# Ending a scatter kernel on Pool: a semaphore wait and a reset of the DMA bookkeeping in place of a drain

## The chip, the cores and the metric

One core of a Trainium2 chip. The time is the device time of one execution, in microseconds (us), median of several executions; the profile's span is 1.8 to 2.2 us shorter than the time of the same execution.

The engines are named as in the profile: PE (TensorE), DVE (VectorE), ACT (ScalarE), Pool (GpSimd) and SP (SyncE); a q after the name is the engine's sequencer. A DMA raises its semaphore, a counter, when it is complete; "landing" in this text is the moment at which an engine's wait for that semaphore is met. The "tail" is the time from the last scatter's landing to the end of the program.

## The reference

```python
def reference(x, scores):               # x: 8 x 2048 x 2560 f32, scores: 8 x 2048 f32
    order = np.argsort(scores, axis=1)
    ranks = np.argsort(order, axis=1)
    out = np.zeros_like(x)
    out[np.arange(B)[:, None], ranks, :] = x
    return out
```

Every row of 10 KB is moved to the place that its score's rank gives it: 168 MB read, 168 MB written, hardly any arithmetic.

## The kernel before

Ranks are counted on VectorE. Most rows go through SBUF: Pool issues a load of 256 rows and, once their ranks are there, two indirect scatters of 128 rows each. The first 256 rows of six batches, and a few others, go straight from DRAM to DRAM in copies of one row, issued by SP and ACT in hardware loops. All synchronization is by hand inside one critical section:

```python
with tc.tile_critical(no_gpsimd_drain=True):
    ...
    def scatters_done(line, k):                  # `line` (an engine) waits for group k's scatters
        i = k % NBUF
        for j in range(GROUPS[BULK[k][1]][1]):
            line.wait(s_scat[i][j], 16 * n_scat[i][j])
    ...
    # SP and ACT: row copies in loops, then each waits for its own
    for line in (sp, act):
        line.wait(s_rows[line], 16 * n_rows[line])
    ...
    for k, (b, g) in enumerate(BULK):            # Pool: 58 groups
        if k >= LAG and k + NBUF - LAG < len(BULK):
            scatters_done(pl, k - LAG)
            load_ahead(k + NBUF - LAG)
        pl.wait(*loaded[k])
        pl.after(dve, t_bulk[b, g])
        for j in range(GROUPS[g][1]):
            scatter(k, j)
    nc.gpsimd.drain()

    for k in range(max(0, len(BULK) - NBUF), len(BULK)):
        scatters_done(sp, k)
```

At the end of the section SP tells the other engines, waits for a drain of ACT, DVE and PE and for a no-op of Pool, and an epilogue with two barriers follows. On Pool that epilogue holds three more drains: a plain one, one with a reset flag over semaphore numbers 132 to 138 (the last not counted, so six numbers), and a plain one.

## Time and profile before

| | before |
|---|---|
| time, median of the first 3 runs | 775.31 us (775.0 to 775.73) |
| span of the profiled run | 772.8 us |
| DMA, mean over the span | 414 GB/s |
| last packet of Pool's DMA queue ends | 770.10 us |
| SP's wait for the last scatter is met | 770.58 us |
| Pool's drain ends | 771.92 us |
| end of the program | 772.80 us |

The first three rows are from the runs and the page; the others are times from the span's start in the trace, in the order in which they end the program. The prediction shows the page's lines and how they are read. What matters is that the DMA engines are full until 766, and that the last 2.23 us (772.801 - 770.575), from the landing of the last scatter to the end, move no data.

### The profile page before, as it was taken

What the parts mean: (1) busy time and instruction counts of PE and PEld (TensorE: products, weight loads), DVE (VectorE), ACT (ScalarE), POOL (GpSimd) and SP (SyncE); (2) the same over time, 40 slices, a digit from 0 to 9 for tenths busy, and PEclk for the clock granted to TensorE, in tenths of its full rate; (3) what the DMA queues carried; (4) which work ended last, traced back from release to release, by engine and by line L of the source; (5) the groups of instructions that cost most, each with busy time, mean ns of one, the idle gap of its engine ahead of it and who ended that gap; (6) DMA issues with size and microseconds to landing.
All of it is one profiled execution on the core that took longest, in us unless ns stands there. A gap on an engine that the chain in (4) does not pass through costs nothing.

```text
span 772.8 us, 8228 instructions
## 1 busy us (share of the span) xinstructions
PE 36.2 (5%) x172; PEld 30.4 (4%) x172; DVE 400.7 (52%) x828; ACT 0.0 (0%) x1; POOL 164.6 (21%) x213
## 2 busy tenths in 40 slices
PE   4000020020020020030000000000000000000000
PEld 3000010010010010030000000000000000000000
DVE  5999979979979979979999500000000000000000
ACT  0000000000000000000000000000000000000000
POOL 4114223222213131312112121212121212112100
PEclk8555555555555555565555555555555555555555
DMA  8999999999999999999999999999999999999996
GB/s 358 418 418 420 418 418 418 418 417 418 418 420 417 420 417 417 419 417 419 416 421 421 422 416 426 416 427 417 422 417 424 417 426 415 424 418 424 419 414 283
DMA packets 80898, 320.15 MB, mean 414 GB/s; under 512 B 28968, under 2 KB 54568, under 8 KB 54568
## 3 DMA queue, kind: packets, MB, share of 16 engines
q0 software_dynamic: 29376, 300.82, 91.7%
q1 hardware_dynamic: 25904, 10.93, 5.2%
q10 hardware_dynamic: 25600, 8.24, 4.3%
q14 instruction: 17, 0.14, 0.0%
q8 instruction: 1, 0.02, 0.0%
HBM read 168.49 MB, written 168.43 MB: 436 GB/s over the span
## 4 chain that ended last, share of the span: by engine, by line
DMA 63%; DVE 13%; another core or an unknown queue 9%; POOL 6%; issue 4%; PE 1%; POOLq 0%; SPq 0%
DMA out_dram<-x,rank_i 57%; DVE trash L239 12%; DMA x<-in_x_dram 6%; POOL out_dram L424 4%; POOL x L126 2%; PE ps_all L196 0%; DVE s_all L341 0%; DMA s_in<-in_scores_dram 0%; PE ps_col L175 0%; POOLq L448 0%; DVE rank_i L277 0%; DVE rank L271 0%; DVE rank L265 0%; PE ps_row L300 0%
## 5 line engine op out<-in xcount | busy, mean ns | idle before, releaser
L239 DVE TENSOR_SCALAR_CACHE_REDUCE trash<-s_all,s_col 128x1792 bf16<-128x1792 f32 (+7 forms) x240 | 315.2, 1348 | 4.6
L424 POOL DMA_INDIRECT out_dram<-x,rank_i x116 | 113.4, 977 | 139.6 <-issue 35.0
L126 POOL DMA_DIRECT2D x<-in_x_dram x88 | 49.4, 565 | 436.9 <-DMA out_dram<-x,rank_i 418.5
L239 DVE SCALAR_TENSOR_TENSOR trash<-s_all,s_col,mask 128x256 bf16<-128x256 f32 x128 | 61.6, 482 | 0.0
L196 PE MATMUL ps_all<-ident,s_col 128*128 128x128 f32 x128 | 28.1, 411 | 3.2 <-DVE s_all L341 2.8
L300 PE MATMUL ps_row<-ident,rank 128*1 128x128 f32 x28 | 8.3, 398 | 393.6 <-DVE rank_i L286 386.4
L196 PEld LDWEIGHTS ps_all<-ident,s_col 128*128 128x128 f32 x128 | 26.5, 222 | 4.2 <-DVE s_all L341 3.2
L341 DVE COPY s_all<-ps_all 128x512 f32<-128x512 f32 x32 | 20.2, 685 | 1.5 <-PE ps_all L196 1.1
L239 DVE DVE_READ_ACCUMULATOR trash<-s_all,s_col 128x1 f32 x240 | 19.9, 83 | 0.0
L300 PEld LDWEIGHTS ps_row<-ident,rank 128*1 128x1 f32 x28 | 2.0, 97 | 397.9 <-DVE rank_i L286 389.5
L311 DVE TENSOR_SCALAR thin_i<-ps_row 1x8 int32<-1x8 f32 x8 | 1.2, 154 | 19.0 <-PE ps_row L300 19.0
L239 DVE DVE_READ_ACCUMULATOR trash<-s_all,s_col,mask 128x1 f32 x128 | 10.7, 83 | 0.0
L326 DVE TENSOR_SCALAR rows_i<-ps_row 1x256 int32<-1x256 f32 x6 | 2.5, 412 | 4.1 <-PE ps_row L300 4.1
L183 DVE COPY s_col<-ps_col 128x128 f32<-128x128 f32 x1 | 0.3, 293 | 4.7 <-PE ps_col L175 4.7
L175 PE MATMUL ps_col<-ident,s_in 8*128 8x8 f32 x16 | 2.1, 262 | 3.9 <-DMA s_in<-in_scores_dram 3.9
L286 DVE TENSOR_SCALAR rank_i<-rank,hole 128x2 int32<-128x2 f32 x8 | 2.1, 262 | 0.3
L175 PEld LDWEIGHTS ps_col<-ident,s_in 8*128 8x128 f32 x16 | 2.0, 211 | 3.9 <-DMA s_in<-in_scores_dram 3.9
L277 DVE CAST rank_i<-rank 128x16 int32<-128x16 f32 (+3 forms) x11 | 1.9, 173 | 0.4
L271 DVE TENSOR_TENSOR rank<-rank,acc 128x16 f32<-128x16 f32 (+3 forms) x11 | 1.9, 171 | 0.4
L265 DVE TENSOR_TENSOR rank<-acc,acc 128x16 f32<-128x16 f32 (+3 forms) x11 | 1.9, 170 | 0.4
L156 POOL TENSOR_SCALAR_AFFINE_SELECT mask<-mask 128x256 f32<-128x256 f32 x2 | 0.8, 398 | 0.0
L168 DVE MEMSET acc<- 128x128 f32 x1 | 0.2, 165 | 1.1 <-SPq L102 1.1
(10 smaller groups left out, 1.8 us busy)
## 6 DMA issues: line engine op xcount, KB each, us to landing
x<-in_x_dram POOLq DMA_DIRECT2D x62, 1280.0 KB
x<-in_x_dram POOLq DMA_DIRECT2D x26, 2560.0 KB
out_dram<-in_x_dram ACTq DMA_DIRECT2D x800, 10.0 KB
out_dram<-in_x_dram SPq DMA_DIRECT2D x800, 10.0 KB
x<-in_x_dram SPq DMA_DIRECT2D x2, 1280.0 KB, 9.1
out_dram<-x,rank_i POOLq DMA_INDIRECT x116, 49.0
s_in<-in_scores_dram SPq DMA_DIRECT2D x1, 64.0 KB
```

What stands on the lines that cost most here:

```text
L126: line.eng.dma_start(out=xb[k % NBUF][:, part], in_=rows[:, part]).then_inc(sem, 16)
L175: nc.tensor.transpose(out=ps_col[:, B * c:B * (c + 1)], in_=s_in[:, r + j:r + m * P:m], identity=ident[:B, :B],)
L196: nc.tensor.transpose(out=ps_all[:, P * c:P * (c + 1)], in_=s_col[:, c, b:b + 1].to_broadcast([P, P]), identity=ident[:],)
L239: do(out=trash[i][:, :P * (hi_c - lo_c)], in0=s_all[:, P * lo_c:P * hi_c], accum_out=acc[i][:, col:col + 1], **how,)
L265: nc.vector.tensor_tensor(out=rank[:, cols], in0=acc[0][:, cols], in1=acc[1][:, cols], op=OP.add)
L271: nc.vector.tensor_tensor(out=rank[:, cols], in0=rank[:, cols], in1=acc[2][:, cols], op=OP.add)
L277: nc.vector.tensor_copy(out=rank_i[:, cols], in_=rank[:, cols])
L286: nc.vector.tensor_scalar(out=rank_i[:, cols], in0=rank[:, cols], scalar1=hole[:, i:i + 1], scalar2=None, op0=OP.add,)
L300: nc.tensor.transpose(out=ps_row[:1, P * j:P * (j + 1)], in_=rank[:, col:col + 1], identity=ident[:],)
L326: nc.vector.tensor_scalar(out=rows_i[b][:].rearrange("o (p j) -> o p j", p=P), in0=ps_row[:1, :WIDE].rearrange("o (j p) -> o p j", p=P), s ...
L341: nc.vector.tensor_copy(out=s_all[:, 512 * q:512 * (q + 1)], in_=ps_all[:, 512 * q:512 * (q + 1)],)
L424: nc.gpsimd.indirect_dma_start(out=out_flat, out_offset=bass.IndirectOffsetOnAxis(ap=rank_i[:, col:col + 1], axis=0), in_=xb[k % NBUF][:, ...
```

## The change

The intent: Pool's drain is still at work when everything has landed. So let Pool wait on the scatters' semaphores itself, and then only reset its DMA bookkeeping.

```diff
             for j in range(GROUPS[g][1]):
                 scatter(k, j)
-        nc.gpsimd.drain()
-
         for k in range(max(0, len(BULK) - NBUF), len(BULK)):
-            scatters_done(sp, k)
+            scatters_done(pl, k)
+
+        nc.gpsimd.dma_reset()
```

The rest of the diff puts the body of the row-copy loop in a function, so that it could be unrolled for the batches of a tuple `FLAT`; `FLAT = ()`, so no batch is, and the instructions are the same. In the built program the reset is a drain instruction with a reset flag over semaphore numbers 96 to 256, that is 160 numbers.

More of the change, by code (lines that the diff above doesn't have):

```diff
@@ L63 @@
     G = 16
+    FLAT = ()
     THIN = {**{(b, 4): 48 for b in range(1, B)}, (7, 5): 44}
@@ L391, with copies @@
                 half = WIDE // 2
-                with line.eng.Fori(0, half // G) as q:
+                def copies(q):
+                    first = b * N + GROUPS[0][0] + half * h
                     _, at = nc.values_load_multi_w_load_instructions(
@@ L402 @@
                     for i in range(G):
-                        row = b * N + GROUPS[0][0] + half * h + i
                         line.eng.dma_start(
                             out=out_bytes[bass.ds(at[i], ROW)],
-                            in_=x_bytes[bass.ds(q * (G * ROW) + row * ROW, ROW)],
+                            in_=x_bytes[bass.ds(q * (G * ROW) + (first + i) * ROW, ROW)],
                         ).then_inc(s_rows[line], 16)
+                if b in FLAT:
+                    for q in range(half // G):
+                        copies(q)
+                else:
+                    with line.eng.Fori(0, half // G) as q:
+                        copies(q)
                 n_rows[line] += half
```

## The prediction

> **What bounds the kernel now.** I read the page first, to see which resource is full and over which part of the span; then the windows of the last microseconds, to see when the data stops; then the few instructions of the epilogue, by their source lines, because the change touches nothing else.
>
> ```profile
> span 772.8 us, 8228 instructions
> DMA  8999999999999999999999999999999999999996
> GB/s 358 418 418 420 418 418 418 418 417 418 418 420 417 420 417 417 419 417 419 416 421 421 422 416 426 416 427 417 422 417 424 417 426 415 424 418 424 419 414 283
> q0 software_dynamic: 29376, 300.82, 91.7%
> HBM read 168.49 MB, written 168.43 MB: 436 GB/s over the span
> ```
>
> The sixteen DMA engines are at nine tenths or more in 38 of 40 slices of 19.3 us, moving a steady 415 to 425 GB/s. DVE is busy 52% and Pool 21%; neither limits anything after the first tenth. The only slices below that are the first (358, the start) and the last (283, the end). A change at the very end can win only in the last slice. The windows there show core time, then five engines' busy time (nothing runs), the clock, the DMA share and GB/s:
>
> ```profile
> 765.50:766.00 0.50, 0.00 (x0) 0.00 (x0) 0.00 (x0) 0.00 (x0) 0.00 (x0) 0.50 0.83 348
> 766.00:766.50 0.50, 0.00 (x0) 0.00 (x0) 0.00 (x0) 0.00 (x0) 0.00 (x0) 0.50 0.29 123
> ...
> 769.50:770.00 0.50, 0.00 (x0) 0.00 (x0) 0.00 (x0) 0.00 (x0) 0.00 (x0) 0.50 0.05 20
> 770.00:770.50 0.50, 0.00 (x0) 0.00 (x0) 0.00 (x0) 0.00 (x0) 0.00 (x0) 0.50 0.00 0
> ```
>
> Full rate lasts until 766.0, a few late DMA engines until 770.0, and then nothing moves: 772.8 - 770.0 = 2.8 us of the span lie behind the last byte. That is all the change can address. What fills those 2.8 us, from the answers on the source lines of the waits on SP (L28), of Pool's drain (L448), of the end of the critical section (L102) and of the program's end (L477); columns: times, duration in ns as min/median/max, first and last start:
>
> ```profile
> L28 SPq EVENT_SEMAPHORE  x8: 27/28/28, 749.6 to 770.6; - x8
> L448 POOLq DRAIN  x1: 32437/32437/32437, 739.5 to 739.5; - x1
> L102 SPq EVENT_SEMAPHORE  x3: 17/28/28, 770.8 to 771.0; - x3
> L102 POOLq NOP  x1: 13/13/13, 772.0 to 772.0; - x1
> L102 SPq NOP  x1: 18/18/18, 772.0 to 772.0; - x1
> L477 POOLq DRAIN  x3: 34/47/72, 772.1 to 772.5; - x3
> L477 PEldq EVENT_SEMAPHORE  x2: 51/51/51, 772.3 to 772.8; - x2
> SPq L102 <- POOLq L102: 0.9, 1, 0.9
> DMA to landing us min/median/max: 29.6/29.6/29.6
> ```
>
> SP's last wait for a scatter is met at 770.6; the last line agrees, since the last scatter was issued at 740.97 and landed 29.6 us later, at 770.6. Pool's drain began at 739.48 (the start that the chain of waits gives for L448) and took 32.437 us, so it ends at 771.92. That is 1.3 us after the last scatter's semaphore was already complete. SP is then the one that waits: 0.9 us for Pool's no-op at the end of the section, from about 771.1 to 772.0. So the drain, not the transfer and not SP, releases the epilogue, and the epilogue from that no-op to the end takes 772.8 - 772.0 = 0.8 us.
>
> **What the Trainium skill says.** "Perfetto Trace Analysis", section "Sequencer-only Instruction (DRAIN, etc)": the profiler's start of such an instruction comes once its semaphores are satisfied, so a recorded duration is execution, not a semaphore wait. This drain has no semaphore, and its 32.4 us are the drain waiting by its own means for what Pool has queued. "PSUM — Partial Sum Buffer", section "Engine vs sequencer instructions": "drain waits for the engine to go fully idle"; the trace agrees as far as it ends only after the last scatter. "DMA: Bandwidth & Descriptors", section "Anatomy of one DMA — SWDGE (gpsimd) path": the semaphore follows only once the last write is confirmed, and this receipt is most of a fixed cost of about 2 us. Here the last bytes are on the DMA engines before 770.0 and the semaphore is seen at 770.6, so the part visible at the end is 0.6 us or little more; the change doesn't touch it. "VectorE: DVE Perf Modes", section "The DRAIN you can't avoid", calls the boilerplate drains some 12 ns on all engines; the trace has 7 to 17 ns on SP, ACT, PE and DVE, but 34 to 72 on Pool, so I use the trace's. No page says what a reset of Pool's DMA bookkeeping costs.
>
> **The change part by part.** The loops over groups, the loads, the scatters and the DRAM-to-DRAM copies are not altered: the tuple of unrolled batches is empty, so every batch takes the loop as before, and the instruction counts on every engine's listing agree but for the epilogue.
>
> Removed: Pool's 32.4 us drain. It lies beside the last transfers but for its last 1.3 us.
>
> Moved: the waits for the last sixteen scatter semaphores go from SP to Pool. In the built program they are eight wait instructions, with the last condition attached to the reset. SP needed 28 ns each, Pool's waits elsewhere show 17 ns. Seven of the eight are met early or with the one that arrives last; at most two or three follow the last landing: 2 to 3 x 17 = 34 to 51 ns, call it 0.05 us. Last semaphore 770.6, so the reset starts at 770.65.
>
> Added: the reset. In the built program it is a drain instruction with a reset flag, over the semaphore numbers 96 to 256. The kernel before already has one such instruction, with the same flag and only the numbers 132 to 138, between its two final barriers: the 72 ns one of Pool's three at L477, against 47 and 34 for the plain ones. If the cost doesn't hang on the range, the reset ends at 770.65 + 0.07 = 770.72.
>
> Freed early: SP no longer waits for scatters, only for its own copies. ACT's copies were complete at 762.1 with the last one issued at 733.2; SP's last was issued at 736.4, so by the same 28.9 us it is through at about 765.3 (an estimate from those rows). The 0.4 us in which SP tells the other engines (770.6 to 771.0) then lies before the last landing, so Pool's no-op finds its condition met. Allow 0.1 us for the branch and fetch between reset and no-op, as from 771.92 to 772.0 now: no-op at 770.82, and the unchanged 0.8 us follow: 771.6.
>
> Sum with a cheap reset: 772.8 - 771.6 = 1.2 us of the span saved, which is 772.0 -> 770.8 at the no-op. The runs' time is longer than the span (775.31 against 772.8, though of different executions), and I take the difference as unchanged.
>
> **The rivals.** (1) The reset costs by the semaphore. The flagged drain took about 72 - 40 = 32 ns more than the plain ones for 6 numbers, 5.3 ns each if all of the difference is due to them; 160 numbers are then 0.85 us. The end would be 0.8 us later than above, a saving of 0.35 us: 774.95. For it speaks only that difference; against it, a second instruction (the range clear, also 72 ns) writes the semaphores themselves. (2) The tail of the drain is real work that has to be done, taking back the ring entries of the scatters, and the reset or the next plain drain does it after all: 1.3 us come back, and the saving is nil or slightly negative, 775.3 to 775.6. For it speaks that the drain ends 1.3 us after all semaphores are in, so it learns of completion in another way; nothing in the trace says whether that is a slow look or work. (3) The drain, while it waits, slows the DMA engines, and its removal speeds up the last 30 us. Against: in the windows from 745 to 765 the DMA share is 1.02 to 1.03 at 408 to 424 GB/s, the same as the 1.02 and 421 from 700 to 720. No gain there. (4) The late DMA engines between 766 and 770 set the end, and their distribution shifts from run to run: that is noise of a fraction of a microsecond, in either direction; the three runs span 775.0 to 775.73, nearly as much as the whole effect.
>
> **Range and chances.** I give 55% to the full 1.2 us, 25% to the half-way reset (0.35), 20% to nothing: 0.66 + 0.09 + 0 = 0.75, and I lean a little toward the full case, the likeliest single one: 0.9 us, so 775.31 - 0.9 = 774.4. The range joins the full saving with a lucky run (774.1 - 0.9 = 773.2) to no saving with an unlucky one (775.8). A change of 2% is 15.5 us; the end has 2.8 us in all to win, so faster by that is next to impossible, 0.5%; slower by it needs a reset of over 16 us, for which nothing speaks but that no page or row bounds it: 1.5%. Within 2%: 98%.
>
> **What would show it.** The page up to the last slice is the same: mean 414 GB/s, DMA-bound. Pool has no drain of tens of microseconds; its waits end with the last landing, 0.6 us or so after the last DMA packet; a reset of about 0.07 us follows, SP is waiting for Pool's no-op since about 766, and from the last landing to the end there are 1.0 us instead of 2.2. A reset of 0.8 us proves rival 1; one of 1.3 us or more, or a long plain drain after it, rival 2. If the GB/s of the last two slices change, rival 3 is at work. The prediction is wrong if the reset takes several microseconds, or if the span falls by more than those 2.8 us.

## The result, and the profile after

| | before | changed |
|---|---|---|
| time, median of 4 runs | 775.2 us | 774.58 us (774.22 to 774.81) |
| span of the profiled run | 772.80 us | 772.35 us |
| wait for the last scatter met | 770.58 us | 771.09 us |
| from there to the end | 2.226 us | 1.260 us |

The ratio is 0.9990, 95% interval 0.9973 to 1.0008. Ratios here are the mean time of one kernel's fast runs over that of the other's fast runs of the same rounds, so not quite the ratio of the medians quoted. An execution counts as slow when it lies over 1.5% above the fastest of its kernel; none here did. Within 2%, and by this interval alone not told apart from no change at all.

The page is the same except at its end (span, DMA share and GB/s in 40 slices, mean):

```profile
span 772.4 us, 8228 instructions
DMA  8999999999999999999999999999999999999997
GB/s 356 420 417 419 417 418 420 417 416 417 420 413 418 418 419 417 418 418 418 417 422 418 424 417 424 416 425 418 426 417 424 417 422 420 420 422 421 420 416 301
DMA packets 80898, 320.15 MB, mean 415 GB/s; under 512 B 28968, under 2 KB 54568, under 8 KB 54568
```

The windows at the end of the changed kernel (same columns as in the prediction):

```profile
769.50:770.00 0.50, 0.00 (x0) 0.00 (x0) 0.00 (x0) 0.00 (x0) 0.00 (x0) 0.50 0.05 20
770.00:770.50 0.50, 0.00 (x0) 0.00 (x0) 0.00 (x0) 0.00 (x0) 0.00 (x0) 0.50 0.05 20
770.50:771.00 0.50, 0.00 (x0) 0.00 (x0) 0.00 (x0) 0.00 (x0) 0.00 (x0) 0.50 0.00 0
```

In this execution the last bytes moved half a microsecond later than in the traced one of before, so the spans differ by less than the tails. The epilogue by source lines, for the waits (L28), the reset (L461), the end of the section (L105), the program's end (L487), and what SP waited for:

```profile
L28 POOLq EVENT_SEMAPHORE  x8: 17/43/43, 751.0 to 771.1; - x8
L461 POOLq DRAIN  x1: 296/296/296, 771.2 to 771.2; - x1
L105 POOLq NOP  x1: 13/13/13, 771.5 to 771.5; - x1
L105 SPq NOP  x1: 18/18/18, 771.6 to 771.6; - x1
L487 POOLq DRAIN  x3: 40/58/64, 771.6 to 772.1; - x3
SPq L105 <- DMA out_dram<-in_x_dram: 31.6, 1, 31.6
SPq L105 <- POOLq L105: 16.6, 1, 16.6
```

The 32 us drain is gone. The eight waits are on Pool, a drain-with-reset of 296 ns follows, and SP has nothing left but to wait 16.6 us for Pool. From the last landing: 0.087 us to the reset's start, 0.296 the reset, 0.044 to Pool's no-op, 0.833 to the end, together 1.260. Before, the same stretch was 1.344 to the end of the drain, 0.045 to the no-op, 0.837 to the end, together 2.226. The tail is 0.97 us shorter.

Twelve runs (seven edited kernels, one of them twice, and both given kernels twice more) then asked three things: is the drain's part after the last landing work or a late look; what does the reset's price hang on; and does the saving in the tail reach the time? All twelve gave correct results.

### The profile page after: what moved, and what is told of

It is laid out like the page before. It is cut to its first block, busy times and chain, and to the rows that moved or that the text cites. A ratio compares the mean times of both kernels' runs of the same rounds, so it can differ in the third digit from the quotient of the medians.

```text
span 772.4 us, 8228 instructions
## 1 busy us (share of the span) xinstructions
PE 35.7 (5%) x172; PEld 30.4 (4%) x172; DVE 400.4 (52%) x828; ACT 0.0 (0%) x1; POOL 165.2 (21%) x213
## 4 chain that ended last, share of the span: by engine, by line
DMA 38%; DVE 37%; another core or an unknown queue 11%; POOL 4%; issue 3%; PE 3%; POOLq 0%; SPq 0%
DVE trash L242 34%; DMA out_dram<-x,rank_i 32%; DMA x<-in_x_dram 6%; POOL out_dram L434 3%; PE ps_all L199 2%; DVE s_all L344 2%; POOL x L129 1%; PE ps_row L303 1%; DMA s_in<-in_scores_dram 0%; PE ps_col L178 0%; DVE rank_i L280 0%; DVE rank L274 0%; DVE rank L268 0%; DVE rank_i L289 0%
```

## The experiments

### Is it the drain itself? A plain drain after the waits, and nothing at all

```diff
 # late_drain
-        nc.gpsimd.dma_reset()
+        nc.gpsimd.drain()
```

> Pool waits for the last scatters as in the changed kernel, then does the old plain drain in place of the reset. Theory A (the drain's 1.3 us after the last semaphore is work that it owes for the queued scatters, taking back their ring entries): the drain still takes 1.0 to 1.4 us after the last landing, the stretch from the last wait's end to the end of the program is about 2.2 us as before, and the time is that of the kernel before, 775.2. Theory B (the drain merely looks late, because it watches by its own means; once all has landed there is nothing to do): it takes 0.03 to 0.1 us, the stretch is 1.0 to 1.1 us, 774.4.

```diff
 # no_reset
-        nc.gpsimd.dma_reset()
```

> Pool waits for the last scatters and then does nothing: no reset and no drain. If the reset's 296 ns are a cost of its own, they go: from the last wait to the end 0.92 us instead of 1.22, 774.3. If they are work for the scatters that somebody has to do, they come back in the first plain drain or in the small flagged drain of the epilogue (58 and 64 ns in the changed kernel), one of which then shows 250 to 300 ns (or 1.3 us by theory A of the plain drain), and the stretch stays at 1.2 us or is longer.

The plain drain of the first, and Pool's three epilogue drains of the second:

```profile
L461 POOLq DRAIN  x1: 2684/2684/2684, 772.0 to 772.0; - x1
```

```profile
L485 POOLq DRAIN  x3: 46/72/2684, 771.9 to 774.9; - x3
```

Everything had landed before either drain started, and it took 2.684 us, to the nanosecond the same in both programs. So theory A holds in kind, with twice the size that I gave it: the drain has work to do, and a late look alone is refuted. With neither drain nor reset the work is not saved; the first plain drain of the epilogue, 58 ns in the changed kernel, does it instead. From the last wait to the end: 3.65 us (late_drain) and 3.71 us (no_reset), against 2.23 before and 1.26 changed.

The times lean the same way. On this chip (number 8), late_drain's median is 777.55 and no_reset's 777.46, with 776.09 for before: some 1.4 us more, as the tails have it (3.65 - 2.23 = 1.42). But the ratios, 1.0014 (0.9993 to 1.0035) and 1.0015 (0.9994 to 1.0036), don't exclude no change; the tails are the evidence. So moving the wait from SP to Pool gains nothing and makes the tail 1.4 us longer by itself: the drain, begun later, can no longer do part of its work beside the transfers. It is the reset that wins.

### What does the reset's price hang on?

```diff
 # small_reset
-        nc.gpsimd.dma_reset()
+        nc.gpsimd.dma_reset(range(132, 138))
```

> The reset covers 6 semaphore numbers (132 to 138) and not 160. If its cost goes by the range, it takes 60 to 80 ns, like the same instruction between the final barriers, instead of 296, and the last wait to the end is 1.0 us. If it goes by what Pool has queued, it stays near 296 ns.

```diff
 # reset_twice
         nc.gpsimd.dma_reset()
+        nc.gpsimd.dma_reset()
```

> Two full resets, one right after the other. If the cost goes by the range, both take about 296 ns. If the first one pays for the scatters' bookkeeping, the second takes 60 to 80 ns. In either case the last wait to the end grows from 1.22 us by the second one's duration, plus 0.04.

The reset of the first, the two resets of the second, and after them Pool's epilogue drains of the first:

```profile
L461 POOLq DRAIN  x1: 73/73/73, 772.0 to 772.0; - x1
```

```profile
L461 POOLq DRAIN  x1: 296/296/296, 771.4 to 771.4; - x1
L462 POOLq DRAIN  x1: 273/273/273, 771.7 to 771.7; - x1
```

```profile
L487 POOLq DRAIN  x3: 40/58/58, 773.7 to 774.4; - x3
```

The price goes by the range: 73 ns for 6 numbers, 296 for 160, or (296 - 73) / 154 = 1.45 ns each if it is linear. Two sizes can't show that it is, nor that the number and not what lies in the range counts. A second full reset, with nothing left to forget, costs 273 ns, so the scatters' bookkeeping made up at most 23 of the first one's 296. And a reset over 6 numbers, none of which any scatter used, relieves the following drains just as well: they take 58 ns at most, not 2684.

The second half of both expectations missed: from the last wait to the end these kernels took 2.77 and 3.46 us, not 1.0 and 1.5. The cause is SP, and is taken up below; in reset_twice another 0.3 us was lost in the last barrier (its no-op to the end takes 1.36 us, 1.05 in small_reset). Their single times, on chip 8, are 776.88 and 776.57.

### What is the drain's work? A drain in the middle

```diff
 # mid_drain, on top of late_drain (mid_drain2: len(BULK) - 2)
             pl.after(dve, t_bulk[b, g])
+            if k == len(BULK) - 4:
+                for i in range(k - NBUF, k):
+                    scatters_done(pl, i)
+                for i in range(k, min(k + NBUF - LAG, len(BULK))):
+                    pl.wait(*loaded[i])
+                nc.gpsimd.drain()
             for j in range(GROUPS[g][1]):
```

> The changed kernel with plain drains: one before the last 4 groups, once everything issued by then has landed (108 scatters, 88 loads), and one at the end after the last 8 scatters. If a plain drain's 2.68 us (twice, in two programs, when begun after all had landed) go by the number of transfers queued since the last one, the first takes about 196/204 x 2.65 = 2.5 us and the last 0.1 to 0.2 us. If they are a fixed price of a drain after any transfer, both take 2.7 us. If they go by the last transfers in the ring alone, the last takes 2.7 us and the first too. The whole kernel is slower by some 40 to 60 us, since Pool stops issuing for a landing; only the two drains' durations are asked.

> As the kernel with a plain drain in the middle, but before the last 2 groups instead of the last 4, so 4 scatters follow instead of 8. Theory E (a plain drain pays about 82 ns for each transfer of Pool's that it still has on its books, and some 45 ns besides): 8 scatters cost 696 ns, so 4 cost 4 x 82 + 43 = 370 ns, and the first drain 2031 + 4 x 82 = 2360 ns, the sum 2.73 us as in the other kernel. Theory F (a fixed price by semaphore, buffer or queue): the last drain stays at about 700 ns.

Middle and last drain, of mid_drain first and of mid_drain2 second:

```profile
L461 POOLq DRAIN  x1: 2031/2031/2031, 747.3 to 747.3; - x1
L467 POOLq DRAIN  x1: 696/696/696, 778.1 to 778.1; - x1
```

```profile
L461 POOLq DRAIN  x1: 2357/2357/2357, 758.6 to 758.6; - x1
L467 POOLq DRAIN  x1: 369/369/369, 776.5 to 776.5; - x1
```

Theory E gave 370 and 2360 ns for the second kernel before it ran, and 369 and 2357 were measured. (696 - 369) / 4 = 82 ns for each scatter (of 128 rows), and 369 - 4 x 82 = 41 ns without any, the size of the epilogue's plain drains. The fixed price is refuted.

By the same rate, the 2684 ns are (2684 - 41) / 82 = 32 transfers, the 2357 ns 28 and the 2031 ns 24: an estimate from these numbers, which takes a load to cost what a scatter does. Pool had queued 204, 200 and 196 transfers by then. So the books grow by one with each transfer queued, and 32 is no upper limit; the first 172 were off them in all three kernels, without a drain, which refutes my first guess in mid_drain of 2.5 us against 0.1 to 0.2. When and how they went is not shown. The kernels themselves are 6.5 and 3.7 us slower than the medians of before on their chips (781.77 on chip 2 and 779.76 on chip 6, one run each), far less than the 40 to 60 that I had put down for the stall, so that guess was wrong too; nothing here uses it.

### How much of it fits beside the last transfers?

```diff
 # drain_two_left, on top of late_drain
         for k in range(max(0, len(BULK) - NBUF), len(BULK)):
+            if k == len(BULK) - 1:
+                nc.gpsimd.drain()
             scatters_done(pl, k)
-
-        nc.gpsimd.drain()
```

> The plain drain begins when all but the last two or three scatters have landed, some 3 to 6 us ahead of the last landing; Pool waits for the last ones after it. If the drain strikes off each transfer as it lands (theory E in order of landing), it has time for the others and ends 0.1 to 0.3 us after the last landing. If a wait inside it costs as in the kernel before, where it began 31 us ahead and ended 1.34 us after the last landing (twice, to 1 ns), it ends about 1.34 us after it again. If it does all of its 2.68 us after the last landing, as when it begins then, 2.7 us.

```profile
L460 POOLq DRAIN  x1: 7372/7372/7372, 765.6 to 765.6; - x1
```

The drain starts at 765.632 and ends at 773.004. The last landing itself isn't seen here, since Pool is in the drain. Pool's last packet ends at 771.193; in the three traces of before the last semaphore is seen 0.47 to 0.48 us after that packet, so the landing here is at about 771.67 and the drain ends some 1.34 us later. That is an estimate: over all the other traces the delay goes from 0.35 (mid_drain2) to 0.71 us (small_reset), which would leave 1.10 to 1.46 us. A drain that begins 6 us ahead of the last landing therefore leaves about as much behind it as one that begins 31 us ahead, and about half as much as one that begins after it. It does not simply strike off each transfer as it lands, or 0.1 us would be left. Why it is about half stays open. The single time is 776.22 us.

### Does it reach the time, and what held up SP?

```diff
 # before_again, before_third: the kernel before, no edit
 # after_again, after_third: the changed kernel, no edit
 # small_again: small_reset once more, no further edit
```

> The kernel before, unedited, for its trace on the chip on which its rivals are looked at. On the last chip three of the four edited kernels had SP's own row copies land at 772 to 773, after the last scatter (771.3 to 771.9), where the first traces have them at 754 to 766. Theory C (how far the copies run behind differs from chip to chip, whatever the end of the program is): here too SP's loop of copies ends later than the first trace's 737, at 745 to 757. Theory D (the edits make the copies late): it ends at 737 as before. In both, Pool's drain ends 1.2 to 1.5 us after the last scatter's landing.

> The changed kernel, unedited, with enough rounds for an interval of some 0.1%. If only the tail has changed (0.97 us between last landing and end in the first two traces), the ratio is 0.9985 to 0.9995 where the scatters land last. Where SP's copies land last, after the scatters, the epilogue of the kernel before has overlapped its drain with that wait, and less is saved: ratio 0.9995 to 1.0005. The reset takes 296 ns again (it did twice in three programs), the last wait to the end 1.22 us if SP is done by then.

> The changed kernel with a reset of 6 numbers. 73 ns for the reset again, so 0.22 us less than the changed kernel from the last wait to the end where SP is done by then, a ratio lower by 0.0003, which 5 rounds may not tell apart; the same time where SP's copies land last.

> The kernel before once more, for its trace on the chip of this call. The drain ends 1.34 us after the last scatter's landing and the last wait's start to the end is 2.23 us, as in the two traces so far; SP's last copy is issued at 736 to 740 on a chip like that of the second call, at 745 to 757 on one like that of the first call.

> The changed kernel again, for a second interval. The tail saves 0.97 us where SP's copies are in before the last scatter: ratio 0.9987 to 0.9995. On a chip where SP's copies land last: 0.9995 to 1.0005.

The first three ran on chip 2, the last two on chip 6. "Tail" is from the start of Pool's (or SP's) last wait for a scatter to the end; "SP in" is when SP's wait for its own copies was over, which in the kernel before is hidden behind its waits for scatters.

| run | chip | time, us | ratio, 95% interval | reset or drain | tail, us | SP in, us |
|---|---|---|---|---|---|---|
| before_again | 2 | 774.97 (1 run) | - | drain, ends 1.345 us after landing | 2.226 | - |
| after_again | 2 | 774.60 (6) | 0.9990, 0.9977 to 1.0003 | 296 ns | 1.259 | 765.7 |
| small_again | 2 | 774.11 (6) | 0.9985, 0.9972 to 0.9997 | 73 ns | 1.031 | 769.0 |
| before_third | 6 | 775.76 (1) | - | drain, ends 1.344 us after landing | 2.226 | - |
| after_third | 6 | 774.93 (5) | 0.9989, 0.9975 to 1.0002 | 296 ns | 2.588 | 773.5 |
| small_reset | 8 | 776.88 (1) | - | 73 ns | 2.771 | 773.4 |

On chip 2 the kernel before had a median of 775.28 (11 runs), on chip 6 776.05 (9 runs). The tail is a fixed quantity as long as SP is in before the last scatter: 2.226 us in all three traces of before, 1.260 and 1.259 changed, 1.031 with the small reset. The small reset saves 0.23 us more than the full one; the 0.49 us between their medians on chip 2 is more than that accounts for, and their intervals overlap, so in time the two are not told apart.

In after_third the traced execution is the slowest of its five (776.93; the others 774.58 to 775.80). Its reset and its end of section, and what SP waited for:

```profile
L461 POOLq DRAIN  x1: 296/296/296, 772.3 to 772.3; - x1
L105 SPq COMPARE_BRANCH  x1: 38/38/38, 773.5 to 773.5; - x1
L105 SPq EVENT_SEMAPHORE  x3: 17/28/28, 773.7 to 773.9; - x3
L105 POOLq NOP  x1: 13/13/13, 773.7 to 773.7; - x1
SPq L105 <- DMA out_dram<-in_x_dram: 24.7, 1, 24.7
```

Here Pool's reset is over at 772.55, but SP leaves its wait for its own row copies only at 773.48; then it tells the others, and Pool's no-op follows at 773.7. In such an execution the row copies end the kernel, and a quicker end on Pool is worth nothing. Pool there waits for SP, where before SP waited for Pool. The same happened in small_reset and reset_twice on chip 8 (SP in at 773.4 and 773.2), which is what their expectations missed.

Why the copies are late in some executions stays open. small_reset and small_again are the same kernel: SP's loop of copies ended at 757.1 in one and at 742.6 in the other, so the end of the program does not set it alone (theory D in that form falls). But the three traces of before have it at 737.1, 739.8 and 739.8, the changed kernel's at 722.8, 738.7 and 748.7, and no trace of before was taken on chip 8. Theory C, that only the chip decides, fails too: on chip 6 it ended at 739.8 (before_third), 738.9 (mid_drain2) and 738.7 (drain_two_left), but at 748.7 in after_third.

### The version with the shortest tail

small_again: wait on Pool, then reset the smallest range that was tried. Of the versions tried it has the shortest tail, 1.03 us against 1.26 and 2.23, and the only interval against before that lies below 1: 0.9985 (0.9972 to 0.9997), 774.11 us. That it beats the changed kernel in time is not shown.

## Why the prediction was right

The time, 774.58, lies 0.18 us from the 774.4 and inside the range. That it came so close is partly luck: the 774.4 is a mean over cases, not the sum of one mechanism (the full case gave 774.1), and runs of one kernel spread over 0.6 to 0.7 us in the result alone. By its steps:

- **The bound, and what is left to win.** Right. Up to the last slice the page is the same, and the gain in the tail came from the stretch after the last landing. Two readings were loose: the full slices move 414 to 427 GB/s and not 415 to 425, and the last packet ends at 770.10 and its semaphore is seen 0.48 us later, not 0.6.
- **The waits, 0.05 us.** 0.087 us from the start of the last wait to the reset; the double-condition waits take 43 ns, not the 17 that I carried over.
- **The reset, 0.07 us.** This term was mis-sized: 0.296 us. I took the price of the flagged drain in the epilogue as independent of its range. Rival 1 had the right cause and too steep a slope (5.3 ns a number where 1.45 were measured), since it charged to the six numbers a difference that is mostly not theirs.
- **Branch and no-op, 0.1 us; epilogue 0.8 us.** 0.044 and 0.833; the first had been 0.045 before too, which the rounding of the rows hid.
- **Sum.** 1.0 us from landing to end was predicted, 1.26 measured in two traces; saved in the tail 1.2 predicted, 0.97 measured; 0.9 in the weighted sum, 0.62 between the medians of the result. The three ratios 0.9990, 0.9990 and 0.9989 agree with about 0.8 us (0.001 of 775), but each interval just reaches past 1, so the tail is the firm evidence.
- **Rival 2**, that the drain's end is real work: right about the work, at 82 ns a transfer and 2.68 us when begun after landing, and wrong that it would come back after a reset. The reset cancels it; without one it does come back, in the epilogue. Whether the work is on ring entries, as the rival had it, no trace shows.
- **Rival 3**, that the drain slows the DMA: no sign of it. From 745 to 765, where the drain of before is waiting, the windows on chip 2 show 419 GB/s with the drain (before_again) and 415 without (after_again), on chip 6 416 and 415. The first traces have 415 and 424, but there the changed kernel's row copies were done at 754 already; that this makes the difference is not shown.
- **SP is through at about 765.3.** A step that holds only for some executions: 754.5, 765.7 and 773.5 in the changed kernel's three traces. I took one trace's pace of the copies as given; where they are late, the saving shrinks or vanishes. That, not the reset, is the largest thing the prediction left out.

## What to carry to other kernels

If an engine's drain ends after the last semaphore of what it drains, ask what it does there: a plain drain on Pool paid for each scatter still on its books, and a wait on semaphores followed by a small reset did away with it. Waiting first and draining then, or leaving the work to the epilogue's drain, made the tail 1.4 us longer, since all of the work moved behind the last landing. And before shortening one chain at a kernel's end, look at when the others end in several executions, because a second chain a microsecond behind takes the gain.

## What the Trainium skill lacked or had wrong

- "PSUM — Partial Sum Buffer", section "Engine vs sequencer instructions", says that a drain waits for the engine to go fully idle. It lacks that on Pool a drain has work of its own after that: 82 ns for each scatter of 128 rows still on the books, 2684 ns here with everything landed.
- No page has the instruction that resets Pool's DMA bookkeeping: 73 ns over 6 semaphore numbers, 296 ns over 160, and either lets the next plain drain end in 58 ns.
- "VectorE: DVE Perf Modes", section "The DRAIN you can't avoid", puts the runtime's boilerplate drains at about 12 ns on all five engines. The drains at the end of this program are its own, so they don't refute that, but the figure does not carry over to them on Pool: SP, ACT, PE and DVE show 7 to 17 ns, Pool 34 to 72 ns.
- "DMA: Bandwidth & Descriptors", section "Anatomy of one DMA — SWDGE (gpsimd) path", makes the write receipt most of a fixed 2 us. Between the end of Pool's last packet and the semaphore seen by the waiting engine, most of these traces show 0.44 to 0.51 us (770.097 to 770.575 in before, 770.633 to 771.090 in the changed kernel, 771.652 to 772.165 in after_third), small_reset 0.71 us (771.221 to 771.926) and mid_drain2 0.35 us (776.024 to 776.376); what lies inside a packet's own duration they don't show.
